# A chunked hybrid layer with expert retrieval: another row list, and the sums of two dense tiles held in PSUM

## The chip, the cores and the metric

The kernel runs on one core of one Trainium2 chip. The metric is the device time of one execution in microseconds. The time before is the median of three runs.

## The reference

One layer over 1024 positions of width 1024, in float32. The front part (modulated norm, an input projection, band attention, a gated delta rule, an output projection) gives the residual stream x1 and the normed input h2 of the last part. The last part is a retrieval over 128 x 128 = 16384 experts, each a single neuron, in blocks of 128 positions:

```python
experts = jnp.take_along_axis(cand_i, pos, axis=-1)      # 8 heads x 16 experts per position
gates = jax.nn.softmax(top_s, axis=-1)
u = expert_down[experts]
vv = expert_up[experts]
act = jax.nn.gelu(jnp.einsum("thkd,td->thk", u, hb), approximate=False)
return jnp.einsum("thk,thkd->td", (gates * act).astype(vv.dtype), vv)
```

The output is x + gate2 * y, with y the sum above.

## The kernel before

The 1024 positions are 8 tiles of 128. The front part goes through lanes of its own (project, delta, attention, output, choose), which a scheduler puts in order by priorities. `choose` gives for each position of a tile the 128 experts and their gates. The retrieval then has two ways.

**Sparse tiles, 0, 1, 6 and 7.** `down(t)` (L893) goes through the 128 slots: GpSimd issues an indirect DMA that gathers one row of 1024 numbers per position (L900), and VectorE multiplies it by h2 and sums it (L902). `up(t)` (L909) gathers the rows of the other table (L914), and VectorE adds each, scaled, to `y` (L919). A row lies in one of 3 buffers, and of 7 once the dense part has opened its pools. `FRONT` names the passes that run beside the front part: down and up of tile 0, down of tile 1. `LATE` names the other five, which run beside the dense part, two at a time where an entry has a third number (`experts`, L1023). GpSimd's queue holds these gathers in the order in which they are issued, and VectorE's queue their sums; both engines work their queues in order.

**Dense tiles, 2 to 5**, 512 positions together. `gates_dense` makes a full table of gates for them and stores it in `gd`. `dense` (L931) then goes through all 128 blocks of 128 experts, four blocks to a step, 32 steps. For a block the table of the down rows is loaded (`rawd`), split into a high part by ScalarE (`dhi`) and a low part by VectorE (`dlo`, L960), and 24 matmuls give the 128 x 512 products `at` (L978). ScalarE takes the Gelu (L981), VectorE multiplies by the gates (L984, tile `g`, loaded for two steps at once, three buffers), ScalarE and VectorE split the result into `whi` and `wlo` (L987, L988). The up rows are split in the same way into `uhi` and `ulo`. After four blocks come the sums: for each of the 4 tiles and 2 halves of 512 columns, 12 matmuls in one PSUM bank of four that take turns (`yc`, L1000), and VectorE adds the bank to `yacc` in SBUF (L1005; in the first step ScalarE copies it, L1003). At the end VectorE multiplies `yacc` by the gate row and adds x1 (L1012, L1013).

The pools of the dense part take the memory of the lanes, which are closed before (L1059); a pool's first tiles wait for that memory.

Of the kernel before, what the change touches and what calls it, by code (L numbers as in the profile page):

```python
# [20 lines left out]
F = mybir.dt.float32  # L21
# [4 lines left out]
AF = mybir.ActivationFunctionType  # L26
OP = mybir.AluOpType
AX = mybir.AxisListType
PSUM = bass.MemoryType.PSUM

P = 128
D = 1024
# [5 lines left out]
PH, TOPK, NK = 8, 16, 128  # L38
# [2 lines left out]
BIG = 1e30  # L41
DENSE = (2, 3, 4, 5)
FRONT = {0: [('d', 0), ('u', 0)], 1: [('d', 1)]}
LATE = [('u', 1, 1), ('d', 6), ('u', 6, 1), ('d', 7), ('u', 7)]
SPARSE = tuple(t for t in range(NT) if t not in DENSE)
CT = len(DENSE)
T = CT * P
SCN = 4
NROW = 3
NMORE = 4  # L50
RINGS = {'P': 4, 'D': 12, 'M': 4, 'O': 3, 'R': 2, 'G': 6}
XBUFS = {'P': 1, 'O': 2}
WBUFS = {'P': 4, 'O': 3}
# [64 lines left out]
def hybrid_layer(ctx, tc, a, out):  # L118
# [770 lines left out]
    def row_tile(name):  # L889
        pools.append(pools.pop(0))  # L890
        return pools[-1].tile([P, D], F, name=name, tag="row")
# [39 lines left out]
    def dense():  # L931
        cx = ExitStack()
        dp = {}
        for n in LAYOUT.split():
            if n.startswith("pad"):
                V.memset(cx.enter_context(tc.tile_pool(name="pad", bufs=1)).tile([P, int(n[3:])], F, name="pad")[:, 0:1], 0.0)
                continue
            dp[n] = cx.enter_context(tc.tile_pool(name=n, bufs=DBUFS[n]))
        acc, wd, upp, hc, gp, dn, rawp = (dp[n] for n in ("acc", "wd", "upp", "hc", "gp", "dn", "rawp"))
        pools.extend([dp["more"]] * NMORE)  # L940
        pyc = cx.enter_context(tc.tile_pool(name="pyc", bufs=4, space=PSUM))
        pat = cx.enter_context(tc.tile_pool(name="pat", bufs=2, space=PSUM))
        yield
        hhi = hc.tile([P, KD, T], R, name="hhi")
        hlo = hc.tile([P, KD, T], R, name="hlo")
        for n in range(CT):
# [2 lines left out]
            SP.dma_start(raw, h2Td[n])  # L949
            A_.activation(hhi[:, :, ts_], raw, AF.Copy)  # L950
            V.tensor_tensor(hlo[:, :, ts_], raw, hhi[:, :, ts_].bitcast(F), OP.subtract)
        yacc = acc.tile([P, CT, D], F, name="yacc")

        def split(pool, tag, src, shape):
            x = rawp.tile(shape, F, name="raw" + tag, tag="raw")
# [7 lines left out]
        for s in range(NK // SCN):  # L963
            if s % 2 == 0:
                hf, i0 = divmod(s * SCN, 64)
                gt = []
                for q in range(2):
                    gt.append(gp.tile([P, CT * 4, 2 * SCN, 16], F, name="g", tag="g"))
                    SP.dma_start(gt[q], gd[q * CT * 4:(q + 1) * CT * 4, hf, :, i0:i0 + 2 * SCN, :].rearrange("b p i n -> p b i n"))
            W, U = [], []  # L970
            for c in range(SCN):
                e = s * SCN + c
                dhi, dlo = split(dn, "d", a["peer_expert_down_t"][e], [P, KD, P])
                ps = pat.tile([P, T], F, name="at", tag="at")
                n = 0
                for l, r in ((dhi, hhi), (dhi, hlo), (dlo, hhi)):
                    for k in range(KD):
                        PE.matmul(ps, l[:, k, :], r[:, k, :], start=(n == 0), stop=(n == 3 * KD - 1))  # L978
                        n += 1
                g = wd.tile([P, T], F, name="gl", tag="gl", bufs=2)  # L980
                A_.activation(g, ps, AF.Gelu)  # L981
                for q in range(2):
                    gq = g[:, q * T // 2:(q + 1) * T // 2].rearrange("p (b n) -> p b n", n=16)
                    V.tensor_tensor(gq, gq, gt[q][:, :, (s % 2) * SCN + c, :], OP.mult)  # L984
                whi = wd.tile([P, T], R, name="whi", tag="whi")
                wlo = wd.tile([P, T], R, name="wlo", tag="wlo")
                A_.activation(whi, g, AF.Copy)  # L987
                V.tensor_tensor(wlo, g, whi.bitcast(F), OP.subtract)  # L988
                W.append((whi, wlo))
                U.append(split(upp, "u", a["peer_expert_up"][e * P:(e + 1) * P, :], [P, D]))  # L990
                yield
            for n in range(CT):
                ts_ = slice(n * P, (n + 1) * P)
                for hf in range(2):
                    cs = slice(hf * 512, (hf + 1) * 512)
                    ps = pyc.tile([P, 512], F, name="yc", tag="yc")
                    m = 0
                    for (whi, wlo), (uhi, ulo) in zip(W, U):
                        for l, r in ((whi, uhi), (whi, ulo), (wlo, uhi)):
                            PE.matmul(ps, l[:, ts_], r[:, cs], start=(m == 0), stop=(m == 3 * SCN - 1))  # L1000
                            m += 1
                    if s == 0:
                        A_.activation(yacc[:, n, cs], ps, AF.Copy)  # L1003
                    else:
                        V.tensor_tensor(yacc[:, n, cs], yacc[:, n, cs], ps, OP.add)  # L1005
                yield
        g2 = gate_row(row_tile("g2c"), 1)
        for n in range(CT):
            t = DENSE[n]
            x1 = row_tile("x1c")  # L1010
            SP.dma_start(x1, x1d[rows_(t)])
            V.tensor_tensor(yacc[:, n, :], yacc[:, n, :], g2, OP.mult)  # L1012
            V.tensor_tensor(x1, x1, yacc[:, n, :], OP.add)  # L1013
            SP.dma_start(out[rows_(t)], x1)
        cx.close()

# [62 lines left out]
```

## Time and profile before

| | |
|---|---|
| median of 3 runs | 3524.43 us (3515.31 to 3529.45) |
| profiled execution | 3538.97 us |
| its span | 3537.0 us |
| TensorE matmul busy | 3016.6 us, 85% |
| VectorE busy | 2783.2 us, 79% |
| ScalarE busy | 1319.4 us, 37% |
| GpSimd busy | 1275.4 us, 36% |
| moved by DMA | 989.72 MB, 280 GB/s over the span |

A busy time is a share of the whole span, over two stages that differ. Matmul durations overlap each other, so two starts tell the pace better than a duration. A wait that is put down to an engine is idle time of the one that waits.

### The profile page before, as it was taken

How to read it: one execution, taken by the hardware profiler on the slowest of the kernel's cores; microseconds unless marked ns; L12 is line 12 of the kernel's file. 1: busy time of each engine (PE TensorE's matmuls, PEld its weight loads, DVE VectorE, ACT ScalarE, POOL GpSimd, SP SyncE). 2: the span in 40 equal slices, each digit the busy share in tenths (PEclk: the TensorE clock that was granted, in tenths of full speed). 3: DMA queues.
4: the chain of work that ended last, by engine and by line, in shares of the span. 5: the costliest groups of instructions: out<-in, count | busy, mean ns of one | idle time of the engine just before them, and what ended most of it. 6: DMA issues, size and time to landing. Idle time of an engine off the chain costs nothing.

```text
span 3537.0 us, 45049 instructions
## 1 busy us (share of the span) xinstructions
PE 3016.6 (85%) x15196; PEld 2478.1 (70%) x15196; DVE 2783.2 (79%) x6529; ACT 1319.4 (37%) x2837; POOL 1275.4 (36%) x1028
## 2 busy tenths in 40 slices
PE   7888768799877898577976699999999998999999
PEld 5677656678756787455856577777777776777777
DVE  3337668758998688974585989999999998888995
ACT  2233134233335763486757532222222222222222
POOL 0000433432333323410000255666556565645540
PEclk9988878899878898786867899999999999999999
DMA  8865787898777987764426799999999999989993
GB/s 284 286 206 168 270 284 266 269 340 277 258 247 237 355 289 268 261 198 133 163 92 223 250 349 343 363 350 353 345 352 350 341 351 336 335 315 316 337 329 105
DMA packets 375960, 989.72 MB, mean 280 GB/s; under 512 B 33440, under 2 KB 139296, under 8 KB 375728
## 3 DMA queue, kind: packets, MB, share of 16 engines
q0 software_dynamic: 147456, 536.94, 42.3%
q1 hardware_dynamic: 228272, 449.90, 37.2%
q8 instruction: 120, 1.97, 0.2%
q14 instruction: 112, 0.92, 0.1%
HBM read 924.84 MB, written 61.87 MB: 279 GB/s over the span
## 4 chain that ended last, share of the span: by engine, by line
PE 30%; DVE 30%; DMA 24%; issue 9%; ACT 6%; POOL 1%; SPq 0%; DVEq 0%; POOLq 0%; ACTq 0%
PE at L978 7%; PE yc L1000 7%; DVE y L919 7%; DVE row L902 7%; DMA g<-gd 6%; PE mm L364 6%; DMA row<-in_peer_expert_down_dram,idx 6%; PE mm L350 4%; DMA row<-in_peer_expert_up_dram,idx 4%; ACT rg L876 2%; DVE ulo L960 2%; DMA w<-in_w_ada_dram 2%; DVE yacc L1005 1%; DVE dlo L960 1%; DVE gl L984 1%
## 5 line engine op out<-in xcount | busy, mean ns | idle before, releaser
L900 POOL DMA_INDIRECT row<-in_peer_expert_down_dram,idx x512 | 640.8, 1252 | 1519.9 <-DVE s L309 359.9
L914 POOL DMA_INDIRECT row<-in_peer_expert_up_dram,idx x512 | 634.4, 1239 | 636.1 <-DVE y L919 213.2
L902 DVE CUSTOM_DVE_ANT_0 row<-row,h2a 128x1024 f32<-128x1024 f32 x512 | 622.2, 1219 | 135.9 <-DMA row<-in_peer_expert_down_dram,idx 132.5
L919 DVE SCALAR_TENSOR_TENSOR y<-row,act,y 128x1024 f32<-128x1024 f32 x508 | 650.3, 1280 | 53.1 <-DMA row<-in_peer_expert_up_dram,idx 51.6
L1000 PE MATMUL yc<-uhi,whi 128*128 128x512 f32 x1024 | 399.2, 402 | 57.6 <-ACT whi L987 39.7
L1000 PE MATMUL yc<-ulo,whi 128*128 128x512 f32 x1024 | 401.6, 398 | 9.1 <-DVE ulo L960 9.1
L1000 PE MATMUL yc<-uhi,wlo 128*128 128x512 f32 x1024 | 361.8, 393 | 5.1 <-DVE wlo L988 5.0
L876 ACT ACTIVATE rg<-rg,gparts 128x128 f16<-128x128 f16 x1024 | 318.5, 395 | 77.4 <-PE mm L877 53.8
L978 PE MATMUL at<-hhi,dhi 128*128 128x512 f32 x1024 | 267.1, 404 | 33.2 <-ACT dhi L959 32.5
L1000 PEld LDWEIGHTS yc<-uhi,whi 128*128 128x128 f32 x1024 | 195.9, 192 | 114.3 <-ACT whi L987 48.9
L364 PE MATMUL mm<-h2T,w 128*128 128x256 f32 (+1 forms) x1280 | 247.2, 354 | 17.2 <-DMA w<-in_peer_w_query_dram 8.0
L978 PEld LDWEIGHTS at<-hhi,dhi 128*128 128x128 f32 x1024 | 198.3, 196 | 84.8 <-ACT dhi L959 41.6
L978 PE MATMUL at<-hlo,dhi 128*128 128x512 f32 x1024 | 256.9, 392 | 0.0
L978 PE MATMUL at<-hhi,dlo 128*128 128x512 f32 x1024 | 255.4, 389 | 0.0
L350 PE MATMUL mm<-w,hT 128*128 128x256 f32 x1024 | 249.0, 398 | 4.6 <-DMA w<-in_w_in_dram 1.6
L364 PEld LDWEIGHTS mm<-h2T,w 128*128 128x128 f32 x1280 | 215.5, 203 | 40.5 <-DMA w<-in_peer_w_query_dram 9.2
L981 ACT ACTIVATE gl<-at 128x512 f32<-128x512 f32 x128 | 76.4, 597 | 435.9 <-PE at L978 435.4
L1000 PEld LDWEIGHTS yc<-ulo,whi 128*128 128x128 f32 x1024 | 196.2, 192 | 53.8 <-DVE ulo L960 13.6
L350 PEld LDWEIGHTS mm<-w,hT 128*128 128x128 f32 x1024 | 199.3, 200 | 42.1 <-issue 6.6
L1000 PEld LDWEIGHTS yc<-uhi,wlo 128*128 128x128 f32 x1024 | 194.3, 190 | 47.3 <-DVE wlo L988 6.8
L978 PEld LDWEIGHTS at<-hlo,dhi 128*128 128x128 f32 x1024 | 194.5, 190 | 41.2
L978 PEld LDWEIGHTS at<-hhi,dlo 128*128 128x128 f32 x1024 | 192.2, 188 | 40.0
(292 smaller groups left out, 5019.5 us busy)
## 6 DMA issues: line engine op xcount, KB each, us to landing
w<-in_w_in_dram SPq DMA_DIRECT2D x140, 512.0 KB
rawd<-_peer_expert_down_t_dram SPq DMA_DIRECT2D x128, 512.0 KB
rawu<-in_peer_expert_up_dram SPq DMA_DIRECT2D x128, 512.0 KB
w<-in_peer_w_query_dram SPq DMA_DIRECT2D x80, 512.0 KB
gd<-stg SPq DMA_DIRECT2D x64, 512.0 KB
g<-gd SPq DMA_DIRECT2D x32, 1024.0 KB
w<-in_w_ada_dram SPq DMA_DIRECT2D x48, 512.0 KB
w<-in_w_out_dram SPq DMA_DIRECT2D x40, 512.0 KB
```

The lines of the kernel that those rows point to most:

```text
L350: PE.matmul(ps[t][:, hf * 256:hf * 256 + 256], hT[:, k, tt * P:(tt + 1) * P], w[k], start=(k == 0), stop=(k == KD - 1), skip_group_check=True)
L364: PE.matmul(ps[:, (c % per) * W:(c % per + 1) * W], w[k][:, (c % 2) * P:(c % 2 + 1) * P], hT[:, k, :W], start=(k == 0), stop=(k == KD - 1) ...
L876: A_.activation(w[:, n, :], oh2[:, n, :], AF.Copy, scale=parts[:, m, n0 + n:n0 + n + 1])
L900: G.indirect_dma_start(out=r, out_offset=None, in_=a["peer_expert_down"], in_offset=bass.IndirectOffsetOnAxis(ap=idx[:, j:j + 1], axis=0))
L902: V.tensor_tensor_reduce(r, r, h2, 1.0, 0.0, OP.mult, OP.add, accum_out=act[:, j:j + 1])
L914: G.indirect_dma_start(out=row, out_offset=None, in_=a["peer_expert_up"], in_offset=bass.IndirectOffsetOnAxis(ap=idx[:, j:j + 1], axis=0))
L919: V.scalar_tensor_tensor(y, row, w[:, j:j + 1], y, op0=OP.mult, op1=OP.add)
L960: V.tensor_tensor(lo, x, hi.bitcast(F), OP.subtract)
L978: PE.matmul(ps, l[:, k, :], r[:, k, :], start=(n == 0), stop=(n == 3 * KD - 1))
L981: A_.activation(g, ps, AF.Gelu)
L984: V.tensor_tensor(gq, gq, gt[q][:, :, (s % 2) * SCN + c, :], OP.mult)
L1000: PE.matmul(ps, l[:, ts_], r[:, cs], start=(m == 0), stop=(m == 3 * SCN - 1))
```

## The change

Four edits. The first pass of `LATE`, the up pass of tile 1, loses its third number and so runs to its end before tile 6's down pass begins. Of the four dense tiles two (`NHELD`) get banks of their own, one for each half of the columns: their matmuls add into these four banks over all 32 steps (`start` in the first step alone, `stop` in the last), and VectorE reads them once, at the end, with the gate row. The other two tiles go through two turning banks in place of four, and `yacc` has half its size. The order of the eight sums of a step alternates between a held and a turning bank. And the pools of the dense part wait for memory tile by tile and not as whole pools.

```diff
-LATE = [('u', 1, 1), ('d', 6), ('u', 6, 1), ('d', 7), ('u', 7)]
+LATE = [('u', 1), ('d', 6), ('u', 6, 1), ('d', 7), ('u', 7)]
...
+NHELD = 2
...
-            dp[n] = cx.enter_context(tc.tile_pool(name=n, bufs=DBUFS[n]))
+            dp[n] = cx.enter_context(tc.tile_pool(name=n, bufs=DBUFS[n], reuse_waits="tile"))
...
-        pyc = cx.enter_context(tc.tile_pool(name="pyc", bufs=4, space=PSUM))
-        pat = cx.enter_context(tc.tile_pool(name="pat", bufs=2, space=PSUM))
+        pyc = cx.enter_context(tc.tile_pool(name="pyc", bufs=2, space=PSUM, reuse_waits="tile"))
+        pyk = cx.enter_context(tc.tile_pool(name="pyk", bufs=1, space=PSUM, reuse_waits="tile"))
+        pat = cx.enter_context(tc.tile_pool(name="pat", bufs=2, space=PSUM, reuse_waits="tile"))
...
-        yacc = acc.tile([P, CT, D], F, name="yacc")
+        held = {(n, hf): pyk.tile([P, 512], F, name=f"yk{n}{hf}") for n in range(NHELD) for hf in range(2)}
+        yacc = acc.tile([P, CT - NHELD, D], F, name="yacc")
...
-            for n in range(CT):
-                ts_ = slice(n * P, (n + 1) * P)
-                for hf in range(2):
+            for i in range(NHELD):
+                for hf, n in ((0, i), (0, i + NHELD), (1, i), (1, i + NHELD)):
+                    ts_ = slice(n * P, (n + 1) * P)
                     cs = slice(hf * 512, (hf + 1) * 512)
-                    ps = pyc.tile([P, 512], F, name="yc", tag="yc")
+                    own = n < NHELD
+                    ps = held[n, hf] if own else pyc.tile([P, 512], F, name="yc", tag="yc")
                     m = 0
                     for (whi, wlo), (uhi, ulo) in zip(W, U):
                         for l, r in ((whi, uhi), (whi, ulo), (wlo, uhi)):
-                            PE.matmul(ps, l[:, ts_], r[:, cs], start=(m == 0), stop=(m == 3 * SCN - 1))
+                            PE.matmul(ps, l[:, ts_], r[:, cs], start=(m == 0 and (s == 0 or not own)),
+                                      stop=(m == 3 * SCN - 1 and (s == NK // SCN - 1 or not own)))
                             m += 1
+                    if own:
+                        continue
+                    ya = yacc[:, n - NHELD, cs]
                     if s == 0:
-                        A_.activation(yacc[:, n, cs], ps, AF.Copy)
+                        A_.activation(ya, ps, AF.Copy)
                     else:
-                        V.tensor_tensor(yacc[:, n, cs], yacc[:, n, cs], ps, OP.add)
+                        V.tensor_tensor(ya, ya, ps, OP.add)
...
-            V.tensor_tensor(yacc[:, n, :], yacc[:, n, :], g2, OP.mult)
-            V.tensor_tensor(x1, x1, yacc[:, n, :], OP.add)
+            if n < NHELD:
+                y = row_tile("yc")
+                for hf in range(2):
+                    cs = slice(hf * 512, (hf + 1) * 512)
+                    V.tensor_tensor(y[:, cs], held[n, hf], g2[:, cs], OP.mult)
+            else:
+                y = yacc[:, n - NHELD, :]
+                V.tensor_tensor(y, y, g2, OP.mult)
+            V.tensor_tensor(x1, x1, y, OP.add)
```

How the instructions move is shown at three places. The first is GpSimd's queue where the down pass of tile 1 ends (its 128 gathers are the first row). Before:

```order
L900 DMA row<-in_peer_expert_down_dram,idx 128x1024 x128
L914 DMA row<-in_peer_expert_up_dram,idx 128x1024
L900 DMA row<-in_peer_expert_down_dram,idx 128x1024
L914 DMA row<-in_peer_expert_up_dram,idx 128x1024
L900 DMA row<-in_peer_expert_down_dram,idx 128x1024
```

And of the changed kernel:

```order
L901 DMA row<-in_peer_expert_down_dram,idx 128x1024 x128
L915 DMA row<-in_peer_expert_up_dram,idx 128x1024 x128
L901 DMA row<-in_peer_expert_down_dram,idx 128x1024 x127
L915 DMA row<-in_peer_expert_up_dram,idx 128x1024
L901 DMA row<-in_peer_expert_down_dram,idx 128x1024 x2
L915 DMA row<-in_peer_expert_up_dram,idx 128x1024 x2
```

Up of tile 1 and down of tile 6 alternated; now they follow each other, and from the last rows on up of tile 6 and down of tile 7 mix as before.

The second place is VectorE's queue behind the last gathered row (the `y<-row,act,y` at the top). Before, the first 12 of its rows:

```order
L919 SCALAR_TENSOR_TENSOR y<-row,act,y 128x1024
L1005 TENSOR_TENSOR yacc<-yacc,yc 128x512
L926 TENSOR_TENSOR g2a<-y,g2a 128x512 x2
L927 TENSOR_TENSOR x1a<-x1a,g2a 128x512
L1005 TENSOR_TENSOR yacc<-yacc,yc 128x512
L927 TENSOR_TENSOR x1a<-x1a,g2a 128x512
L988 TENSOR_TENSOR wlo<-gl,whi 128x512
L960 TENSOR_TENSOR ulo<-rawu,uhi 128x1024
L1005 TENSOR_TENSOR yacc<-yacc,yc 128x512
L960 TENSOR_TENSOR ulo<-rawu,uhi 128x1024 x2
L960 TENSOR_TENSOR dlo<-rawd,dhi 128x1024
L984 TENSOR_TENSOR gl<-gl,g 128x256 x2
```

Of the changed kernel, with `yk` the held banks:

```order
L920 SCALAR_TENSOR_TENSOR y<-row,act,y 128x1024 x2
L964 TENSOR_TENSOR ulo<-rawu,uhi 128x1024
L927 TENSOR_TENSOR g2a<-y,g2a 128x512 x2
L988 TENSOR_TENSOR gl<-gl,g 128x256 x2
L928 TENSOR_TENSOR x1a<-x1a,g2a 128x512 x2
L992 TENSOR_TENSOR wlo<-gl,whi 128x512
L1025 TENSOR_TENSOR yc<-yk_18124,g2c 128x512
L1014 TENSOR_TENSOR yacc<-yacc,yc 128x512
L1025 TENSOR_TENSOR yc<-yk_18125,g2c 128x512
L1014 TENSOR_TENSOR yacc<-yacc,yc 128x512
```

Before, 64 instructions stood behind the last row, with five more splits of down rows among them; now 23 stand there, and the last block's products (`gl`, `wlo`) are the first of them.

The third place is TensorE's queue where a turning bank is taken again. Of the changed kernel, in the middle of the dense part, with buffer numbers: 21757 and 21809 are the same bank, one step's first and third sum of the tiles that are not held.

```order
L1005 MATMUL yk00_18124<-uhi_21741,wlo_21736 128x512
L1005 MATMUL yc_21757<-uhi_21741,wlo_21736 128x512
L1005 MATMUL yk01_18125<-uhi_21741,wlo_21736 128x512
L1005 MATMUL yc_21783<-uhi_21741,wlo_21736 128x512
L1005 MATMUL yk10_18126<-uhi_21741,wlo_21736 128x512
L1005 MATMUL yk11_18127<-uhi_21741,wlo_21736 128x512
L982 MATMUL at_21855<-hhi_18106,dhi_21851 128x512 x3
L982 MATMUL at_21855<-hlo_18107,dhi_21851 128x512 x8
L982 MATMUL at_21855<-hhi_18106,dlo_21852 128x512 x8
L1005 MATMUL yc_21809<-uhi_21606,whi_21600 128x512
```

Before, a bank was taken again by the fourth sum after it; now by the second of the two tiles, with held sums and the next block's `at` matmuls between.

## Rows read from the trace of the kernel before

**Rows 1.** Busy time by engine in three stretches; clock, DMA share and GB/s last.

```profile
core 0: us, PE busy (x) PEld busy (x) DVE busy (x) ACT busy (x) POOL busy (x), PEclk, DMA share, GB/s
1550.00:1988.00 438.00, 318.70 (x1917) 264.03 (x1916) 269.94 (x1082) 302.12 (x872) 8.48 (x8) 0.75 0.46 156
1988.00:3452.00 1464.00, 1367.21 (x5802) 1104.40 (x5803) 1339.92 (x1764) 392.04 (x498) 842.27 (x631) 0.97 0.95 341
3452.00:3537.00 85.00, 77.78 (x344) 64.06 (x342) 45.56 (x59) 20.35 (x26) 0.00 (x0) 0.98 0.28 96
```

**Rows 2.** Instructions of L978 and of L1000: durations, first and last start.

```profile
L978 PE MATMUL at<-hhi,dhi x1024: 387/389/796, 1987.9 to 3504.7; 128*128 128x512 f32 x171
...
L1000 PE MATMUL yc<-uhi,wlo x1024: 387/389/628, 2005.8 to 3529.4; 128*128 128x512 f32 x171
```

**Rows 3.** The chain that ended last, 3440 us on: start, duration, what.

```profile
3483.08 10.88 PE yc L1000 x48
```

**Rows 4.** VectorE's groups, 1988 to 3452 us: busy, mean ns | idle before, releasers.

```profile
L919 DVE SCALAR_TENSOR_TENSOR y<-row,act,y 128x1024 f32<-128x1024 f32 x380 | 486.7, 1281 | 1.8 <-DMA row<-in_peer_expert_up_dram,idx 0.6
L902 DVE CUSTOM_DVE_ANT_0 row<-row,h2a 128x1024 f32<-128x1024 f32 x252 | 305.7, 1217 | 0.4 <-DMA row<-in_peer_expert_down_dram,idx 0.4
L1005 DVE TENSOR_TENSOR yacc<-yacc,yc 128x512 f32<-128x512 f32 x231 | 151.2, 679 | 22.1 <-PE yc L1000 22.1
```

**Rows 5.** Who waited for whom, 1988 to 3452 us: us in total, times, longest.

```profile
POOL row L900 <- DVE y L919: 166.4, 100, 10.9
POOL row L914 <- DVE act L902: 156.1, 91, 10.0
POOL row L914 <- DVE y L919: 125.3, 81, 10.1
...
DVE gl L984 <- DMA g<-gd: 74.9, 15, 8.8
...
PEld at L978 <- ACT dhi L959: 41.6, 24, 8.5
...
PE yc L1000 <- ACT whi L987: 39.7, 19, 4.5
PE at L978 <- ACT dhi L959: 32.5, 20, 8.3
...
DVE yacc L1005 <- PE yc L1000: 22.1, 20, 4.0
...
PE yc L1000 <- DVE yacc L1005: 13.7, 10, 2.6
```

**Rows 6.** Instructions of L1005 and of L1003, whole span.

```profile
L1005 DVE TENSOR_TENSOR yacc<-yacc,yc x248: 672/680/690, 2075.9 to 3529.8; 128x512 f32<-128x512 f32 x124
...
L1003 ACT ACTIVATE yacc<-yc x8: 577/600/632, 2036.4 to 2048.5; 128x512 f32<-128x512 f32 x8
```

**Rows 7.** VectorE in order of time, from 2605 us: start, duration, instruction.

```profile
2606.29 1.21 DVE L960 TENSOR_TENSOR dlo<-rawd,dhi 128x1024 fp32r<-128x1024 f32 x1
2607.42 1.21 DVE L902 CUSTOM_DVE_ANT_0 row<-row,h2a 128x1024 f32<-128x1024 f32 x1
...
2609.71 0.68 DVE L1005 TENSOR_TENSOR yacc<-yacc,yc 128x512 f32<-128x512 f32 x1
2610.31 1.27 DVE L919 SCALAR_TENSOR_TENSOR y<-row,act,y 128x1024 f32<-128x1024 f32 x1
2611.51 1.21 DVE L902 CUSTOM_DVE_ANT_0 row<-row,h2a 128x1024 f32<-128x1024 f32 x1
```

**Rows 8.** DMA of 1988 to 3452 us; then the gathers' queue, whole span.

```profile
DMA packets 191530, 499.22 MB, mean 341 GB/s; under 512 B 14704, under 2 KB 77711, under 8 KB 191449
...
q0 software_dynamic: 147456, 536.94, 42.3%
```

**Rows 9.** The page's GB/s in 40 slices of 88.4 us.

```profile
GB/s 284 286 206 168 270 284 266 269 340 277 258 247 237 355 289 268 261 198 133 163 92 223 250 349 343 363 350 353 345 352 350 341 351 336 335 315 316 337 329 105
```

**Rows 10.** Two stretches of 50 us; columns as in rows 1.

```profile
2200.00:2250.00 50.00, 49.91 (x219) 40.47 (x218) 49.99 (x67) 13.34 (x17) 32.67 (x25) 1.00 0.95 352
2700.00:2750.00 50.00, 47.70 (x211) 39.15 (x210) 50.00 (x70) 12.97 (x16) 32.30 (x25) 1.00 0.96 352
```

**Rows 11.** The chain that ended last, 1900 us on: three loads of gate tiles.

```profile
2069.71 20.22 DMA g<-gd
2165.24 18.93 DMA g<-gd
...
2741.35 19.23 DMA g<-gd
```

## The prediction, made before the changed kernel ran

> **What bounds the kernel now.** I read the busy time by stretch first, because the page's averages mix two stages. Up to 1988 us the front work runs and every engine has gaps; in its last part, 1550 to 1988 us, the DMA engines are busy 46% and GpSimd issues almost nothing [rows 1]. The dense stage begins with the first `at` matmul at 1987.9 us [rows 2]. From there to 3452 us, where VectorE finishes the last gathered row, three resources are nearly full at once: DMA 0.95 of its time at 341 GB/s, VectorE 1339.92 of 1464 us (92%), and TensorE 1367.21 us (93%, at a granted clock of 0.97) [rows 1]. After 3452 us only dense work is left: the DMA share is 0.28, TensorE is busy 77.78 of 85 us [rows 1]. So the change has to be judged on the 1549 us from 1988 us to the end of the span. I count its work in steps: one step is four experts, 4 x 24 `at` and 8 x 12 `yc` matmuls, 192 in all, 32 steps.
>
> A busy TensorE is not TensorE at its peak here: 48 matmuls back to back took 10.88 us [rows 3], 0.2267 us each, so all 6144 need 1393 us. The stretch to 3452 us did 5802 matmuls [rows 1], 30.2 steps at 48.5 us, where the matmuls alone need 43.5.
>
> VectorE is the engine that the others wait for. GpSimd's gathers wait for it to give rows back (166.4, 156.1 and 125.3 us in three groups), while VectorE almost never waits for a row: 1.8 and 0.4 us before its 632 large row operations [rows 4, 5]. Its own 124 idle us (1464 less 1339.92) are mostly 74.9 us, 15 times, for the gate tiles `g`, and 22.1 us for sums that TensorE had not finished [rows 4, 5]. When VectorE is late, ScalarE's `whi` and then TensorE are late: TensorE waits 39.7 us for `whi`, 32.5 for `dhi` (there a transfer was late), 13.7 for a `yc` bank [rows 5].
>
> **The change, part by part.** Durations are those of the profiled execution, 3538.97 us with a span of 3537.0; the median of the runs is 3524.43, 14.5 us less, and I shift the result by that.
>
> *Sums held in PSUM.* Tiles 0 and 1 of the dense four no longer go through VectorE once per step. Of 248 additions [rows 6] 124 go, and 4 of 8 first copies on ScalarE (0.600 us each [rows 6], at one step, where ScalarE has room). Between two starts such an addition takes 0.60 us (2609.71 to 2610.31) [rows 7]: 124 x 0.60 = 74 us less VectorE work. Waits of VectorE for `yc` should halve, 11 us. At the end four multiplications of 512 columns, read from PSUM, stand for two of 1024: 4 x 0.60 against 2 x 1.13 (a 1024-column operation steps by 1.13 us [rows 7]), nothing.
>
> *Row list.* The five row passes stay in number. Tile 1's up pass goes first and alone, and the order of instructions lets only three rows of it run before the dense stage, where before six rows ran: 637 in place of 634 (632 and two first ones that are plain multiplications), 3 x 1.17 = 4 us more VectorE work in the stage and 1.6 MB more to move (536.94 MB over 1024 rows, 0.524 MB each [rows 8]). Each pass now has all seven row buffers when it is alone; the queue is GpSimd's alone and nothing else stands in it. The idle 1550 to 1988 us stays idle.
>
> *Where the rows end.* Before, 64 VectorE instructions follow the last row; now 23. The rows are spread over nearly all steps: about 120 matmuls, 27 us, should remain behind the last row, then 8 us for last sum, product and store as now (3529.4 to 3537) [rows 2], together 35 us in place of 85.
>
> *Two turning banks for four.* A bank's reuse has to wait for its addition. In the order some 29 matmuls (6.6 us) lie between a bank's last matmul and its next first one, against 39 (8.8 us) before, with half as many additions queued on VectorE. The wait is between nothing and what it was, 13.7 us; I take that as unchanged.
>
> *Pool waits by tile.* They can only bring the first dense loads forward. The first 16 `at` matmuls now stand ahead of the last eight gate matmuls: 0 to 10 us gained; I take 0, since gate tiles of the last dense tile must still be written and read back.
>
> **The sum.** Three paths for the 1549 us:
> - VectorE: 1339.92 + 45.56 busy, - 74 + 4, + 124 of waits - 11 = 1428, and about 20 for the last matmuls: 1448.
> - TensorE: 1393, + 42 for late `dhi` (its longer row, on the weight side [rows 5]), + 8 at the end: 1443.
> - DMA: 499.22 MB [rows 8], + 8.2 in the last 85 us (96 GB/s), + 1.6, less 3.4 that the last 35 us carry: 506 MB. At 341 / 0.95 = 359 GB/s, if it never paused, 1408 + 35 = 1443; at the 341 seen, 1483 + 35 = 1518. The first ten full slices of the dense stage, from the 349 to the 351 of the page [rows 9], have a mean of 350: 1445 + 35 = 1480.
>
> Before, VectorE's path was the longest and held the other two back; now all three lie within a few us of 1445 and wait for each other in turn, so the slowest at its realistic rate counts: DMA at 350 GB/s, **1480 us, 69 less**. That is 46.0 us per step. 3524 - 69 = **3455 us**.
>
> **A rule of the Trainium skill, weighed.** The gathers wait for VectorE and not the other way round [rows 4, 5], so I hold VectorE for the resource that sets DMA's rate. The Trainium skill (Perfetto Trace Analysis, Identifying the Most-Contended Engine) says to take the engine with the highest utilization as the one to improve. By that, DMA at 0.95 is the bound, no byte is saved, and relief for VectorE gives only the better-filled end; this is the first rival.
>
> **Rivals.**
> 1. *DMA's rate stays.* The transfers are the bound already and 341 GB/s is what they give with this mix of small and large packets. For it: 0.95 busy. Against it: in 2200 to 2250 us VectorE was busy 49.99 of 50 us and in 2700 to 2750 us 50.00 [rows 10], so it had nothing to spare there. 1518 us, -31: 3493 us. Chance 0.14.
> 2. *The gate tiles take it back.* Of three `g` buffers two are in use, so the second load of a pair is issued only when VectorE has done the last product of the pair before; it then needs some 19 us (20.22, 18.93, 19.23 [rows 11]), and VectorE, in order, stands. A VectorE with less work reaches that point sooner and waits longer. If all that is saved goes there, the pace stays 48.5 us per step: 31.4 x 48.5 + 35 = 1558, +9: 3533 us. Against it: a pair of steps loses 8 additions, 4.8 us, of which only those that stand between the last product and the next can turn into waiting. Chance 0.14.
> 3. *Two banks are too few: slower.* TensorE, in order, stands before a bank until its addition is done, and the addition stands in VectorE's queue behind a product that waits for `g`. Two reuses per step, 64, at 1.37 us each (13.7 over 10 [rows 5]) are 88 us, and 15 waits of 5.0 us (74.9 over 15) that now pass on to TensorE 75 more: 1480 + 163, 3618 us. It decides from 69 / 64 = 1.1 us per reuse on. For it: TensorE has only 1549 - 1393 = 156 us of slack in all. Against it: the 29 matmuls of distance, and six of eight banks open at once to take an expert's products as they come. The Trainium skill (Perfetto Trace Analysis, Matmuls) speaks for this rival: independent groups should rotate through different PSUM banks so that the evacuation of one lies beside the next. The runs of before show that price only as 13.7 us with four banks. Chance 0.10.
> 4. *The row list does more than the order says*, and tile 1's rows run in the idle 438 us before the dense stage. 125 rows, 65 MB, would leave DMA's path, TensorE's 1443 would remain: -106, 3418 us. Against it: the order pins their VectorE instructions behind the first dense ones. Chance 0.02.
>
> **How the numbers follow.** My forecast, any pace between the three bounds and 47 us per step, has 0.60; its own range is 3410 to 3490. 0.5%, 18 us, is about what a measurement of this kernel can tell from no change: faster is below 3507, slower above 3542. Faster: 0.60 + 0.14 + 0.02 = 0.76; same: 0.14; slower: 0.10. The low end is the bound of 1443 with 10 us at the start, 3524 - 116, rounded to 3410; the high end, 3530, leaves out rival 3 and about half of rival 2.
>
> **What would show it.** In the changed profile: the additions at 124 or so, about 75 us; VectorE's busy share of the dense stage down to some 89%, with the wait for `g` still 15 or 16 times; last row within 40 us of the end; 46 us per step; GB/s in the stage near 350 to the end instead of falling to 315 to 337. The forecast is wrong if GB/s stays at 341 (rival 1), if the wait for `g` grows from 75 to beyond 150 us (rival 2), or if TensorE's wait for the additions grows from 13.7 us to over 60 (rival 3).

## The result and the profile after

| | before | changed kernel |
|---|---|---|
| median | 3529.9 us (14 runs) | 3500.87 us (14 runs, 3479.86 to 3515.26) |
| ratio | | 0.9907, 95% interval 0.989 to 0.9925 |
| profiled execution | 3538.97 us | 3495.83 us |
| its span | 3537.0 us | 3494.1 us |

The ratio puts the gain at 0.93%, 33 us of 3530 (the two medians are 29 us apart), where 69 were forecast. Gains in us below are worked out from the ratios in this way. The time lies inside the forecast range, but a little under half of the gain came, so the mechanism has to be looked at. Busy time of the changed kernel by stretch, cut at its first `at` matmul and behind its last gathered row (against [rows 1]):

```profile
core 0: us, PE busy (x) PEld busy (x) DVE busy (x) ACT busy (x) POOL busy (x), PEclk, DMA share, GB/s
1550.00:1967.00 417.00, 310.38 (x1877) 255.81 (x1875) 256.60 (x1040) 297.98 (x860) 8.85 (x3) 0.77 0.46 154
1967.00:3472.00 1505.00, 1424.05 (x6099) 1161.08 (x6100) 1314.28 (x1711) 409.00 (x521) 869.17 (x634) 0.98 0.94 336
3472.00:3494.00 22.00, 13.00 (x55) 9.76 (x53) 15.75 (x22) 0.63 (x1) 0.00 (x0) 0.89 0.50 191
```

The middle stretch did 6099 matmuls, 31.8 steps, in 1505 us: **47.4 us per step**, where 48.5 stood before and 46.0 were forecast. VectorE is busy 1314 of 1505 us, 87%, so it was relieved and has gaps. But DMA did not go faster, as it should have with VectorE out of the way: 336 GB/s after 341. The ends are as good as forecast or better: 22 us behind the last row, and the dense stage begins 21 us earlier:

```profile
L982 PE MATMUL at<-hhi,dhi x1024: 387/389/796, 1967.2 to 3466.7; 128*128 128x512 f32 x171
...
L1014 DVE TENSOR_TENSOR yacc<-yacc,yc x124: 674/683/689, 2058.1 to 3486.9; 128x512 f32<-128x512 f32 x124
L1012 ACT ACTIVATE yacc<-yc x4: 575/590/600, 2013.9 to 2025.9; 128x512 f32<-128x512 f32 x4
```

Half of the 248 additions and of the 8 copies are gone [rows 6]. What VectorE does with the time is seen in its groups from 1967 to 3472 us (busy, mean ns | idle before, releasers; against [rows 4]):

```profile
L964 DVE TENSOR_TENSOR dlo<-rawd,dhi 128x1024 fp32r<-128x1024 f32 x128 | 156.2, 1220 | 25.8 <-ACT dhi L963 25.7
L964 DVE TENSOR_TENSOR ulo<-rawu,uhi 128x1024 fp32r<-128x1024 f32 x128 | 156.1, 1221 | 39.3 <-ACT uhi L963 39.3
L988 DVE TENSOR_TENSOR gl<-gl,g 128x256 f32<-128x256 f32 x254 | 98.3, 423 | 78.4 <-DMA g<-gd 39.1 <-ACT gl L985 39.0
...
L1014 DVE TENSOR_TENSOR yacc<-yacc,yc 128x512 f32<-128x512 f32 x120 | 80.0, 683 | 30.9 <-PE yc L1005 30.4
```

And in the waits of the same stretch (us in total, times, longest; against [rows 5]):

```profile
ACT dhi L963 <- DMA rawd<-_peer_expert_down_t_dram: 66.8, 23, 7.1
...
PE yk L1005 <- ACT whi L991: 56.4, 27, 5.2
ACT uhi L963 <- DMA rawu<-in_peer_expert_up_dram: 51.7, 18, 8.5
...
DVE ulo L964 <- ACT uhi L963: 39.3, 19, 8.3
DVE gl L988 <- DMA g<-gd: 39.1, 13, 8.7
```

VectorE's wait for the gate tiles fell from 74.9 to 39.1 us. In its place VectorE stands 65 us (25.7 + 39.3) before the low parts of the raw tables, because ScalarE had not split them yet; for 60 us of the 65 ScalarE itself was waiting for the table to land. TensorE waits 56.4 us for `whi`, up from 39.7. Late tables as such are nothing new. Before (1988 to 3452 us), ScalarE waited longer for them than now, 152.7 us against 118.5, but VectorE stood only 11.7 us behind it:

```profile
ACT dhi L959 <- DMA rawd<-_peer_expert_down_t_dram: 112.1, 48, 9.5
...
ACT uhi L959 <- DMA rawu<-in_peer_expert_up_dram: 40.6, 19, 10.7
...
DVE dlo L960 <- ACT dhi L959: 6.1, 6, 1.8
DVE ulo L960 <- ACT uhi L959: 5.6, 5, 2.0
```

The chain that ended last says which transfers these are. From 2100 us on it goes through eleven loads of raw tables of 13 to 20 us, about one for each pair of steps (start, duration, what); four of them:

```profile
2148.35 18.78 DMA rawu<-in_peer_expert_up_dram
...
2329.92 20.30 DMA rawd<-_peer_expert_down_t_dram
...
2526.57 19.30 DMA rawd<-_peer_expert_down_t_dram
2621.28 6.71 DMA g<-gd
2627.99 19.10 DMA rawu<-in_peer_expert_up_dram
```

The chain of before, from 1990 us on, had two raw tables of 13 us or more and eleven gate loads, of which three are shown [rows 11]. Both raw tables were issued right behind two gate loads; the longer one:

```profile
2357.97 22.14 DMA rawu<-in_peer_expert_up_dram
```

So VectorE's stall moved from the gate tiles to the tables queued behind them. SyncE's queue at one of the four (start, duration of the issue):

```profile
2325.93 3.90 SPq L973 DMA_DIRECT2D g<-gd  x2
2329.92 5.81 SPq L960 DMA_DIRECT2D rawd<-_peer_expert_down_t_dram  x1
2335.83 0.38 SPq L960 DMA_DIRECT2D rawu<-in_peer_expert_up_dram  x1
2344.20 0.33 SPq L960 DMA_DIRECT2D rawd<-_peer_expert_down_t_dram  x1
```

A gate tile is 1 MB, read from `gd` in pieces of 8 x 16 floats, 512 bytes. The down table issued right behind two such loads takes 5.81 us to issue, where 0.33 is usual, and 20.30 us to land, where the same chain has 8.96 us for an up table at 2026.13. The other places are alike: from 2000 us on, the fifteen raw tables issued right behind gate loads took 2.4 to 16.7 us to issue (median 11.7); for all other raw tables the median is 0.33 us.

### The profile page after: what moved, and what is told of

Its sections match the earlier page's. It is cut to its first block, busy times and chain, and to the rows that moved or that the text cites. A ratio compares the mean times of both kernels' runs of the same rounds, so it can differ in the third digit from the quotient of the medians.

```text
span 3494.1 us, 44943 instructions
## 1 busy us (share of the span) xinstructions
PE 3014.0 (86%) x15196; PEld 2482.1 (71%) x15196; DVE 2719.5 (78%) x6407; ACT 1316.2 (38%) x2833; POOL 1310.2 (37%) x1028
## 4 chain that ended last, share of the span: by engine, by line
PE 37%; DMA 26%; DVE 20%; issue 9%; ACT 5%; POOL 3%; SPq 0%; DVEq 0%; POOLq 0%; ACTq 0%
PE at L982 12%; DMA row<-in_peer_expert_down_dram,idx 8%; PE yk L1005 6%; PE mm L365 5%; PE yc L1005 4%; DVE row L903 4%; DMA row<-in_peer_expert_up_dram,idx 4%; DMA rawu<-in_peer_expert_up_dram 4%; DVE y L920 4%; PE mm L351 3%; DMA rawd<-_peer_expert_down_t_dram 2%; POOL row L901 2%; DMA g<-gd 2%; ACT rg L877 2%; DMA w<-in_w_ada_dram 1%
## 5 line engine op out<-in xcount | busy, mean ns | idle before, releaser
L915 POOL DMA_INDIRECT row<-in_peer_expert_up_dram,idx x512 | 664.5, 1298 | 1035.5 <-DMA g<-gd 421.3
L920 DVE SCALAR_TENSOR_TENSOR y<-row,act,y 128x1024 f32<-128x1024 f32 x508 | 651.8, 1283 | 53.3 <-DMA row<-in_peer_expert_up_dram,idx 50.1
L1005 PE MATMUL yk<-uhi,whi 128*128 128x512 f32 x512 | 202.5, 412 | 61.7 <-ACT whi L991 56.4
L351 PEld LDWEIGHTS mm<-w,hT 128*128 128x128 f32 x1024 | 199.2, 200 | 45.3 <-DMA w<-in_w_in_dram 6.4
L1005 PE MATMUL yk<-ulo,whi 128*128 128x512 f32 x512 | 204.0, 404 | 3.5 <-DVE ulo L964 3.5
L1005 PE MATMUL yc<-uhi,whi 128*128 128x512 f32 x512 | 205.1, 401 | 0.5 <-DVE yacc L1014 0.5
L1005 PE MATMUL yc<-ulo,whi 128*128 128x512 f32 x512 | 204.2, 399 | 0.0
L1005 PE MATMUL yc<-uhi,wlo 128*128 128x512 f32 x512 | 199.5, 390 | 0.0
L870 DVE TENSOR_TENSOR rg<-iota_n,gkeys 128x1024 f16<-128x1024 f16 x128 | 151.0, 1222 | 55.9 <-PE mm L878 55.8
```

What stands on the lines that cost most here:

```text
L351: PE.matmul(ps[t][:, hf * 256:hf * 256 + 256], hT[:, k, tt * P:(tt + 1) * P], w[k], start=(k == 0), stop=(k == KD - 1), skip_group_check=True)
L870: V.tensor_tensor(oh, iota_n[:, None, :].to_broadcast([P, GQ, P]), keys[:, key, n0:n0 + GQ, None].to_broadcast([P, GQ, P]), OP.is_equal)
L915: G.indirect_dma_start(out=row, out_offset=None, in_=a["peer_expert_up"], in_offset=bass.IndirectOffsetOnAxis(ap=idx[:, j:j + 1], axis=0))
L920: V.scalar_tensor_tensor(y, row, w[:, j:j + 1], y, op0=OP.mult, op1=OP.add)
L1005: PE.matmul(ps, l[:, ts_], r[:, cs], start=(m == 0 and (s == 0 or not own)), stop=(m == 3 * SCN - 1 and (s == NK // SCN - 1 or not own)))
```

## The experiments

Theory G: the held sums bring what was forecast, and the row list gives half of it back, by way of the gate loads: tables queued behind their small pieces are late. Rivals: D, the DMA's rate is the bound whatever VectorE does (rival 1); P, two turning banks are too few (rival 3); T, the tile waits or the list do something of their own. Ratios are to the kernel before on the same chip, with 95% intervals. The last column counts raw tables and gate loads of 13 us or more in the chain that ended last, from 1990 us on.

| run | ratio | us per step | GB/s | late: raw, gate |
|---|---|---|---|---|
| before | 1 | 48.5 | 341 | 2, 11 |
| changed kernel | 0.9907 (0.989 to 0.9925) | 47.4 | 336 | 11, 2 |
| e1, row list alone | 0.9952 (0.9931 to 0.9974) | 47.5 | 339 | 1, 6 |
| e2, held sums alone | 0.9833 (0.9797 to 0.987) | 46.4 | 349 | 4, 5 |
| e4, old row list | 0.983 (0.9803 to 0.9857) | 46.2 | 349 | 5, 3 |
| e5, fourth gate buffer | 0.9876 (0.9848 to 0.9903) | 47.1 | 338 | 10, 0 |
| e6, gates in 4-KB pieces | 0.9701 (0.9651 to 0.9751) | 45.1 | 352 | 2, 0 |
| e7, 124 additions put back | 1.0085 (1.006 to 1.011) | 47.0 | 319 | 11, 0 |
| e8, half of each raw table | 0.9936 (0.9908 to 0.9964) | 48.0 | 303 | 2, 4 |
| e9, gates loaded once | 0.9608 (0.9558 to 0.9659) | 44.1 | 348 | 0, 0 |
| e11, old list, 8-KB pieces | 0.9762 (0.9738 to 0.9786) | 45.3 | 356 | 0, 0 |
| e12, changed, 8-KB pieces | **0.9732** (0.9708 to 0.9756) | 45.1 | 353 | 1, 0 |
| e13, gate loads from ScalarE | 0.9907 (0.9885 to 0.9928) | 47.0 | 339 | 0, 9 |

Steps and GB/s are of the stretch from the first `at` matmul to the last gathered row of each run's profile, time over matmuls by 192. (In e7 the rows end last; its stretch ends with the last matmul.)

**e1: the row list alone,** on the kernel before.

```diff
-LATE = [('u', 1, 1), ('d', 6), ('u', 6, 1), ('d', 7), ('u', 7)]
+LATE = [('u', 1), ('d', 6), ('u', 6, 1), ('d', 7), ('u', 7)]
```

> The kernel before with the new row list alone (the four yc banks, all sums on VectorE as before). In the order 35 VectorE instructions follow the last row in place of 64, and the first at matmuls stand ahead of the last eight gate matmuls. Theory A (the transfers of the dense stage run at some 340 GB/s whatever VectorE does): the better-filled end and the earlier start carry the change's gain, so most of it is here: -20 to -30 us, ratio 0.991 to 0.994. Theory C (VectorE's work is the bound, as forecast): the list takes no work from VectorE, so only the earlier start of about 20 us in the changed kernel's trace would come, ratio 0.994 to 0.997.

The list by itself is a small gain, 0.5%, 17 us: the dense part starts at 1978.1 us instead of 1987.9, and 37 us are left behind the last row instead of 85. Its pace is 47.5 us per step, where before had 48.5. The ratio lies in the range of theory C.

**e2: the held sums alone,** the changed kernel with the old list and whole-pool waits.

```diff
-LATE = [('u', 1), ('d', 6), ('u', 6, 1), ('d', 7), ('u', 7)]
+LATE = [('u', 1, 1), ('d', 6), ('u', 6, 1), ('d', 7), ('u', 7)]
...
-            dp[n] = cx.enter_context(tc.tile_pool(name=n, bufs=DBUFS[n], reuse_waits="tile"))
+            dp[n] = cx.enter_context(tc.tile_pool(name=n, bufs=DBUFS[n]))
...
```

> The kernel before with the held sums and the two turning banks alone (old row list, pools waiting as whole pools). Theory C: 124 additions less on VectorE, -50 to -75 us, ratio 0.979 to 0.986. Theory A: the rate stays near 340 GB/s, so -5 to -15 us, ratio 0.996 to 0.999.

-59 us, near the forecast's -69, with two turning banks. It lies in the range of theory C.

**e4: the changed kernel with the old list** (tile waits kept).

```diff
-LATE = [('u', 1), ('d', 6), ('u', 6, 1), ('d', 7), ('u', 7)]
+LATE = [('u', 1, 1), ('d', 6), ('u', 6, 1), ('d', 7), ('u', 7)]
```

> The changed kernel with the old row list: as the run with held sums alone, but pools wait for memory tile by tile. The order of every engine is the same as in that run; some fifteen waits differ. If these waits matter at all, the first at matmul starts earlier, by up to 10 us; otherwise the same time within 0.2%.

0.983, the same as e2: with the old list, tile waits do nothing that can be measured. Its stretch is the forecast almost to the digit, 46.2 us per step at 349 GB/s:

```profile
1982.00:3416.00 1434.00, 1380.53 (x5961) 1126.71 (x5961) 1290.33 (x1664) 398.97 (x505) 846.19 (x631) 0.99 0.97 349
3416.00:3465.00 49.00, 41.79 (x185) 34.27 (x183) 28.35 (x37) 11.21 (x14) 0.00 (x0) 0.95 0.35 129
```

So on top of the held sums the row list costs 0.0077, 27 us, though alone it gains 17 (e1). The waits of this stretch say where: VectorE stands 21 us before the low parts, where the changed kernel has 65, and that is nearly all of the difference in its idle time (144 us here, 191 there).

```profile
DVE ulo L964 <- ACT uhi L963: 17.4, 14, 3.5
...
DVE dlo L964 <- ACT dhi L963: 3.6, 9, 1.1
```

D falls in its plain form: the same transfers go at 349 GB/s with one list and at 336 with the other. In e4's SyncE queue the down table stands before the gate loads, and the up table behind them is the late one:

```profile
2337.37 0.33 SPq L960 DMA_DIRECT2D rawd<-_peer_expert_down_t_dram  x1
2343.57 4.26 SPq L973 DMA_DIRECT2D g<-gd  x2
2347.93 14.20 SPq L960 DMA_DIRECT2D rawu<-in_peer_expert_up_dram  x1
2362.22 0.50 SPq L960 DMA_DIRECT2D rawd<-_peer_expert_down_t_dram  x1
```

Over the whole queue: in the kernel two gate loads serve a pair of steps, eight experts, and the queue holds the second load of a pair and the first of the next side by side. With the old list (e4) they stand behind the down table of that pair's second expert in all fifteen places from the second pair on; in the changed kernel they stand ahead of it in six of the fifteen, and four of these six are the four places where the chain goes through a late `rawd`. The list alone does not do this: in e1 they stand behind that down table in all fifteen places, as before. The order changed only where list and held sums came together.

**e5: a fourth gate buffer,** on the changed kernel (`hc=1, gp=3` to `gp=4`).

> The changed kernel with four buffers for the gate tiles in place of three (the memory that half of yacc freed), so that both loads of a pair of steps can be issued a pair ahead. Theory A (rate): no byte less, as the changed kernel, 0.988 to 0.993 of before. Theory B (once per pair of steps the two gate loads, 2 MB in pieces of 512 bytes, hold up the raw tables behind them on SP's queue, and VectorE's freed time goes into that wait): the wait for g (39 us) goes, but the raw loads still stand behind the gate loads; 0.975 to 0.985.

VectorE's wait for `g` falls from 39.1 to 2.0 us, and the kernel gains 0.3% if anything (the intervals overlap); theory B's 0.975 to 0.985 did not come. ScalarE now waits 89.6 us for `rawd` and 65.0 for `rawu` from 2000 to 3400 us, where the changed kernel has 58.5 and 50.1:

```profile
ACT dhi L963 <- DMA rawd<-_peer_expert_down_t_dram: 89.6, 25, 8.6
ACT uhi L963 <- DMA rawu<-in_peer_expert_up_dram: 65.0, 19, 9.1
...
DVE gl L988 <- DMA g<-gd: 2.0, 1, 2.0
```

The gate load is not late any more, and what stands behind it still is.

**e6: the same bytes of gates in 4-KB pieces.** Other gates are read than those that belong to the experts, and the first pairs' gate loads stand earlier in SyncE's queue; the rest of the order is that of the changed kernel but for a few instructions.

```diff
-                    SP.dma_start(gt[q], gd[q * CT * 4:(q + 1) * CT * 4, hf, :, i0:i0 + 2 * SCN, :].rearrange("b p i n -> p b i n"))
+                    SP.dma_start(gt[q].rearrange("p (c b) i n -> p c (b i n)", c=2), gd[2 * q:2 * q + 2, hf].rearrange("b p i n -> p b (i n)"))
```

> The changed kernel with gate tiles loaded from a contiguous stretch of the same array: as many bytes and loads, in pieces of 4 KB in place of 512 bytes (other gates are read, so the dense tiles' products are those of other experts). Theory A (rate by bytes): unchanged, 0.988 to 0.993 of before. Theory B (the gate loads hold up the raw tables behind them): the raw tables that land some 18 to 20 us after issue in the changed kernel's chain come earlier, 0.972 to 0.982.

-73 us against the changed kernel, at equal bytes, somewhat more than theory B said. From 2000 us on, the raw tables behind gate loads take 0.33 to 0.51 us to issue.

**e7: 124 additions put back.** VectorE adds a spare 128 x 512 tile to another in each place where a held sum saved an addition.

```diff
                     if own:
+                        if s:
+                            V.tensor_tensor(junk, junk, hjunk, OP.add)
                         continue
```

> The changed kernel with the 124 additions put back on VectorE as additions of 128x512 in SBUF that nothing waits for and that wait for nothing but VectorE. Theory C (VectorE's work still sets the pace): +60 to +75 us against the changed kernel, 1.007 to 1.012 of before. Theories A and B (VectorE has 191 us of waiting in the changed kernel's dense stage): at most +20 us, 0.990 to 0.996.

+63 us against the changed kernel, as theory C said: VectorE's work still costs nearly its full time (74 by the forecast's price). The scheduler laid the gathered rows later, though, so the loss shows as a tail of 70 us without a matmul, and not as a slower step, and the 63 us are the price of the additions and of the new order together (the first stretch here starts 9 us ahead of the first `at` matmul):

```profile
1967.00:3482.00 1515.00, 1432.57 (x6168) 1171.69 (x6167) 1336.93 (x1833) 418.54 (x541) 870.37 (x593) 0.97 0.91 319
3482.00:3552.00 70.00, 0.00 (x0) 0.00 (x0) 66.47 (x57) 0.00 (x0) 42.96 (x42) 0.51 0.98 376
```

**e8: half of each raw table.** Half of the 512 KB is loaded and used twice, so the products are of other numbers; VectorE and ScalarE do the same work.

```diff
-            x = rawp.tile(shape, F, name="raw" + tag, tag="raw")
-            SP.dma_start(x, src)
+            x = rawp.tile([P, 512], F, name="raw" + tag, tag="raw")
+            if len(shape) == 3:
+                SP.dma_start(x.rearrange("p (a b) -> p a b", b=P), src[:, 0:4, :])
+            else:
+                SP.dma_start(x, src[:, 0:512])
```

> The changed kernel with raw tables loaded by half (512 of 1024 columns, read twice by ScalarE and VectorE, so the dense tiles' results are not the reference's): 67 MB less in the dense stage, instructions and loads unchanged in number. Theory A (rate by bytes): 506 - 67 = 439 MB at 336 GB/s is 1307 us, below TensorE's 1443, so the stage falls to some 1445 to 1460, -45 to -60 against the changed kernel, 0.973 to 0.978 of before. Theory B: the half tables still stand behind the gate loads, -10 to -25 us, 0.983 to 0.988.

This run decides nothing. 67 MB less (256 tables by 0.262 MB) gave no gain, 0.9936, outside the ranges of both theories. Taken alone that would speak against D. But the order changed with it: the last row starts at 3407.5 us and the last matmul at 3499.9.

**e9: gate tiles loaded once.** The gates of the first pair of steps serve all 32.

```diff
-            if s % 2 == 0:
+            if s == 0:
```

> The changed kernel with the gate tiles loaded once, for the first pair of steps, and used for all 16 (other gates are read, so the dense tiles' products are wrong): no gate load after the first two, 31.5 MB less. Theory A (rate by bytes): 31.5 MB at 336 GB/s are 94 us, cut short by TensorE's 1443: -60 to -80 against the changed kernel, 0.968 to 0.974. Theory B: the whole price of the gate loads, about as much as with contiguous pieces plus the wait for g of 39 us.

-106 us against the changed kernel, 44.1 us per step at 348 GB/s, near the 43.5 that the matmuls alone need. That is about the whole price of the gate loads, bytes, pieces and waits together (the order moved too), and near theory B's sum, the 73 us of e6 plus the 39 us wait for `g`.

**e11 and e12: the gate table in another layout,** so that a gate tile is one run of 8 KB per partition; the store, in the front part, now writes 512-byte pieces. e11 has the old list, e12 the new one; all engines' instructions keep the order of e4 and of the changed kernel.

```diff
-    gd = tc.dram_tile([CT * 8, 2, P, 64, 16], F, name="gd")
+    gd = tc.dram_tile([2, 64 // (2 * SCN), P, CT * 8, 2 * SCN, 16], F, name="gd")
...
-                SP.dma_start(gd[DENSE.index(t) * 8 + blk, hf], stg[:, hf * 64:hf * 64 + 64, :])
+                SP.dma_start(gd[hf, :, :, DENSE.index(t) * 8 + blk].rearrange("c p i n -> p c (i n)"),
+                             stg[:, hf * 64:hf * 64 + 64, :].rearrange("p (c i) n -> p c (i n)", i=2 * SCN))
...
-                    SP.dma_start(gt[q], gd[q * CT * 4:(q + 1) * CT * 4, hf, :, i0:i0 + 2 * SCN, :].rearrange("b p i n -> p b i n"))
+                    SP.dma_start(gt[q], gd[hf, i0 // (2 * SCN), :, q * CT * 4:(q + 1) * CT * 4])
```

> Held sums with the old row list, and the gate table laid out so that a gate tile is one run of 8 KB per partition for the load (the store then writes 512-byte pieces in the front part). All outputs are computed as in the reference. The order of all five engines' instructions is that of the run with the old list (ratio 0.983). Theory 1 (the raw tables wait on SP's queue behind the gate loads' 512-byte pieces): in that order the second expert's down table is always issued ahead of the gate loads, so the gain is smaller than the 65 us that contiguous gates gave on the new list: 25 to 50 us, ratio 0.969 to 0.976, and the stage's rate stays near 350 GB/s or above. Theory 2 (the row passes themselves set the pace, the gate loads cost every list the same): 65 us, ratio 0.965 or less. If the small pieces only move their cost into the front part, the first at matmul starts later than 1982 us by 10 us or more.

> The changed kernel with the gate table laid out so that a gate tile is one run of 8 KB per partition for the load. All outputs are computed as in the reference. The order of all five engines' instructions is that of the changed kernel (ratio 0.991). Theory 1: raw tables no longer land 18 to 20 us after their issue, the 27 us by which the new list is behind the old one go: within 10 us of the run with the old list and the same layout, ratio 0.967 to 0.974, 45.5 us per step or less. Theory 2: it stays some 27 us behind that run, ratio near 0.973 where that has 0.965. Where the store's 512-byte pieces cost the front part something, both kernels pay it and their difference still counts.

The layout gains 24 us with the old list (25 to 50 were expected) and 62 with the new one, and the new list's arrears of 27 us are gone: 0.9732 against 0.9762, a lead of 11 us, if anything (the intervals just overlap). This is the test that tells G from T: with order and bytes the same, the list's cost went with the small pieces. The issue times say the same: from 2000 us on, each of the fifteen raw tables behind gate loads takes 0.33 us to issue in both runs. e12's stretch, its SyncE queue at the same place, and the one long raw table left in its chain:

```profile
1983.00:3416.00 1433.00, 1401.29 (x6099) 1150.53 (x6100) 1313.61 (x1711) 409.41 (x521) 869.38 (x634) 0.99 0.95 353
```

```profile
2327.96 0.80 SPq L974 DMA_DIRECT2D g<-gd  x2
2329.71 0.33 SPq L961 DMA_DIRECT2D rawd<-_peer_expert_down_t_dram  x1
2332.59 0.33 SPq L961 DMA_DIRECT2D rawu<-in_peer_expert_up_dram  x1
```

```profile
2609.61 15.17 DMA rawu<-in_peer_expert_up_dram
```

The matmuls (6099) and VectorE's work (1313.61 us) are those of the changed kernel, in 72 us less. The two gate loads are issued in 0.80 us, and the down table behind them in 0.33. The layout's price should stand in the front part: ScalarE waits 43.7 us for stores of `stg` from 1200 to 2000 us, where it waited 17.0, and the dense part begins at 1983.5 us, 16 later. How much of these 16 us the stores make is not shown: with the old list the wait grew from 27.3 (e4) to 36.5 us (e11), and the dense part began 3 us earlier. e12 is the best version here that computes the whole layer, 95 us faster than before.

**e13: the gate loads from ScalarE's queue,** pieces of 512 bytes as before.

```diff
-                    SP.dma_start(gt[q], gd[q * CT * 4:(q + 1) * CT * 4, hf, :, i0:i0 + 2 * SCN, :].rearrange("b p i n -> p b i n"))
+                    A_.dma_start(gt[q], gd[q * CT * 4:(q + 1) * CT * 4, hf, :, i0:i0 + 2 * SCN, :].rearrange("b p i n -> p b i n"))
```

> The changed kernel with the gate tiles' loads issued by ScalarE instead of SyncE, in the same 512-byte pieces; VectorE's, GpSimd's and ScalarE's other instructions keep nearly the changed kernel's order. All outputs are computed as in the reference. If the raw tables are late because they stand behind a gate load on the same queue, they are now on another queue: ratio 0.975 to 0.984 (against 0.991), fewer raw tables of 13 to 20 us in the chain that ended last than the changed kernel's 10 or more. If the small pieces slow all transfers, whatever queue they are on, nothing is gained: ratio 0.988 or more, and the raw tables stay late. Against a gain: the second load of a pair waits for VectorE's last product of the pair before, and on ScalarE it now holds up ScalarE's splits and Gelus; if that decides, ratio above 0.995 and TensorE's waits for dhi and whi grow.

No gain in sum, where G had 0.975 to 0.984. Its waits (2000 to 3400 us) show why this is not a plain failure of G:

```profile
DVE gl L988 <- DMA g<-gd: 61.0, 10, 8.7
...
ACT dhi L963 <- issue: 48.1, 7, 12.8
...
ACT dhi L963 <- DMA rawd<-_peer_expert_down_t_dram: 14.9, 7, 3.8
...
ACT uhi L963 <- DMA rawu<-in_peer_expert_up_dram: 2.2, 2, 1.4
```

On another queue than the gate loads the raw tables are no longer late: ScalarE's waits for them in the same window fell from 58.5 and 50.1 us to 14.9 and 2.2, and no raw table of 13 us is left in the chain. What was gained went to two other waits: ScalarE stands 48.1 us before `dhi` behind its own issue of a gate load, and VectorE waits 61.0 us for `g`. So place in the queue decides who is late; that somebody is late goes with the pieces (e6, e11, e12). The Trainium skill (DMA: Bandwidth & Descriptors, Issuing engines are not separate DMA queues) says that issuing from several engines saves only sequencer time; the total agrees (0.9907 twice), the waits show that it still changes which transfer is late.

## Where the prediction failed, and where it held

The step that failed is the term of the row list, valued at 4 us of VectorE work and no wait; on top of the held sums it cost 27 us. One of the prediction's own signs of being wrong appeared with it: GB/s did not rise from 341 (336).

1. *Sums held in PSUM: right.* 124 additions went, and with the old list (e2, e4) the kernel gained 59 and 60 us where the sum said 69: 46.2 us per step for 46.0, 349 GB/s for 350. That these 350 GB/s are a limit, as the sum took them, is not shown: e11 moves the same bytes at 356. e7 prices the work from the other side, 63 us for 124 additions and the order that came with them.
2. *Row list: the step that failed.* It was valued at nothing beyond 4 us of VectorE work: "Each pass now has all seven row buffers when it is alone; the queue is GpSimd's alone and nothing else stands in it." That looked at GpSimd's queue only. With list and held sums together the scheduler also laid SyncE's queue anew, and there the gate loads came ahead of raw tables that are needed at once. On top of the held sums it cost 27 us (e4 against the changed kernel), 1.2 us per step and 13 GB/s. Shown: the cost goes when the gate loads' pieces are large (e11, e12), and the tables' lateness goes when they are on another queue (e13). Not shown: that the place of the `rawd` is the whole of it. Of the 44 us more that VectorE stands before low parts than in e4, 22 are for down tables and 22 for up tables; seven of the eleven late tables are up tables, which are late with the old list as well (five), and no run moved a single load by hand. Why the list alone gains on the kernel before fits in with this: in e1 the gate loads keep their place in SyncE's queue, and before, VectorE was the last to arrive, so that a late table held up ScalarE (152.7 us) and hardly VectorE (11.7). It was not tested apart.
3. *The ends: better than taken.* Row list and tile waits were given 0 at the start; the dense part began 21 us earlier, and 22 us instead of 35 stood behind the last row. e1 starts 10 us earlier, and e2 and e4, without and with the tile waits, 6 and 6. Which edit brings how much cannot be told from this, since the runs built on the changed kernel with its list and gate layout (e5 to e9, e13) start anywhere from 1968 to 1981 us. Against the forecast's sum there are 60 us more in the middle stretch (42 by the pace, 18 because it holds more of the matmuls), 13 less behind it, 21 less at the start, together 26, by which the profiled execution missed its 3470.
4. *Two turning banks: right.* TensorE's matmuls waited 0.5 us for a bank's addition, twice, after 13.7 us (rival 3 needed over 60).
5. *Rival 1 has the time, not the reason.* 3493 us was its forecast, and GB/s "stays at 341" came true (336). But the rate is not what the engines can carry: with larger pieces the same work moved at 353 (e12). The rule of the Trainium skill that the prediction weighed (Perfetto Trace Analysis, Identifying the Most-Contended Engine) asks for HBM utilization and not for the occupancy of the DMA engines, and the 0.95 it was given was that occupancy; 0.94 to 0.97 stands in runs of 336 to 353 GB/s alike, so the occupancy told nothing here.
6. *Rival 2 had the place.* The gate loads did take the gain back, not through VectorE's wait for `g`, which fell to 39.1 us, but through the tables behind them. The prediction read the loads of 19 and 20 us [rows 11] as something that only VectorE waits for, and did not ask what else stands on that queue. The chain of before had an answer that [rows 11] left out, an up table issued right behind two gate loads that took 22.14 us. The Trainium skill (Perfetto Trace Analysis, DMA Optimizations) warns of DMAs under 2 KB for their overhead. The trace agrees in direction: 73404 of the changed kernel's 181791 packets from 2000 to 3400 us are under 2 KB, 14680 of e12's 132229, and e12 moved 356 GB/s there for 339. With the old list the same pieces moved at 351 GB/s (e4) and the large ones at 356 (e11), so the pieces by themselves make the smaller part of the difference.

## What to carry to other kernels

Gains that were measured one by one do not add: held sums -59, row list -17, both -33. When an engine is relieved, look at the next late transfer and at everything that stands behind it on the same queue, and read all queues of the new order, not only that of the engine the edit names. A load in small pieces was a stall for whatever was queued behind it; a layout that makes its reads long, at the cost of short writes in the front part, was worth more on top of the change (62 us) than the change itself (33).

## What was not expected of the hardware

Two 1-MB loads in 512-byte pieces took 3.90 and 4.26 us to issue, and the 512-KB load behind them 5.81 and 14.20 us, against 0.80 and 0.33 us with pieces of 8 KB (medians of the fifteen loads behind, from 2000 us on: 11.7 us in the changed kernel, 0.33 in e12). The busy share of the DMA engines does not show this: 0.94 with the small pieces at 336 GB/s, 0.95 with the large ones at 353. And a load moved to a queue of its own (e13) freed those behind it, but then the engine that issued it stood: 48.1 us on ScalarE in seven waits.
